# Two transformer layers on one core: paced bias blocks, softmax scaling and low weight parts on other engines, new step orders

## The chip, the cores and the metric

The kernel runs on one NeuronCore of a Trainium2 chip. Its engines work side by side, each on a queue of its own: TensorE (PE, matrix products into PSUM; its weight loads are PEld), VectorE (DVE), ScalarE (ACT), GpSimd (POOL) and SyncE (SP, which here only issues DMAs). They wait for each other by semaphores. The metric is the device time of one launch in microseconds (us), the median over several runs.

## The reference

Two layers over 512 latent tokens and 256 context tokens of width 1024 (`DEPTH = 2`). Layer 0 mixes tokens by differential attention (8 heads), layer 1 by neighbourhood attention (16 heads, a window of 8 rows by 16 columns of the token grid, with a learned bias per relative position, and all context tokens). Each is followed by an MLP. Context tokens go the same way, except after the last layer.

```
for i in range(DEPTH):
    mod_l = jnp.split((jax.nn.silu(c) @ w_mod[i] + b_mod[i])[:, None, :], N_MOD, axis=-1)
    mod_c = jnp.split((jax.nn.silu(c_ctx) @ w_mod[i] + b_mod[i])[None, None, :], N_MOD, axis=-1)
    h_l = modulate(rms_norm(x, norm1_g[i]), mod_l[0], mod_l[1])
    h_c = modulate(rms_norm(ctx, norm1_g[i]), mod_c[0], mod_c[1])
    ...
    x = x + mod_l[2] * y_l
    x = x + mod_l[5] * squared_relu_mlp(modulate(rms_norm(x, norm2_g[i]), mod_l[3], mod_l[4]), w_mlp1[i], w_mlp2[i])
    ...

# neighbourhood_mixer, one row of queries (layer 1)
s_loc = jnp.einsum('bqhd,brkhd->bhqrk', q_row, k_band).astype(jnp.float32) * ATTN_SCALE
bias = rpb[:, row_off][:, :, col_bias_idx].transpose(0, 2, 1, 3)
s_loc = jnp.where(col_in[None, None, :, None, :], s_loc + bias[None].astype(jnp.float32), -jnp.inf)
s_ctx = jnp.einsum('bqhd,bkhd->bhqk', q_row, k_c).astype(jnp.float32) * ATTN_SCALE
prob = jax.nn.softmax(jnp.concatenate([s_loc.reshape(...), s_ctx], axis=-1), axis=-1)
```

## The kernel before

**Products in parts.** Every large product is made of three PE passes over split operands: a value is held as a high part, which ACT copies from the raw float32 into the rounded type, and a low part, the difference between the two. `wraw` (L125) issues the DMA of a raw weight piece on SP, `wsplit` (L135) makes the high part on ACT (L140) and the low part on POOL unless another engine is named (L141). Raw pieces go through two buffers R.

**Stages.** After a start that sets up modulation and the first head, layer 0's eight heads run until about 434 us of the profile, then its output projection until about 550, its MLP until about 1176, layer 1's attention in eight groups of two heads until about 1547, its projection until about 1582, and its MLP to the end.

**Order of the work.** In the attention stages PE, SP and POOL keep the order in which the code is written; that order comes from strings of steps. `run` walks a string: `w` fetches a weight piece for the next head or group, `c` splits it, `Q` is the query, key and value product and its normalisation, `U` the transposes of queries and keys, `S` the scores with the softmax, `T` the transposes of the probabilities, `V` the product with the values. A prime marks the head or group before the one that is being begun. `P`, `X`, `B` belong to the output projection: a step of it, the split of a head's attention output, the gates. `m` and `n` are the modulation of the next layer. CYCLE1 is the string of layer 1's groups, LAST1 that of the last, END0 and END1 are the ends of the two attention stages. Elsewhere a scheduler orders instructions by its own estimate.

**Layer 1.** `group1` has the steps: `qk_normed` (a power of the mean square on POOL at L287, then the product with it on DVE at L414), `turn` (U: L623, L625, splits at L427 to L441), `scores` (S: products L645, bias added at L648, maximum L651, exponential L652, and the two halves scaled by the reciprocal of their sums on DVE, L656), `turned` (T: L675, high part L676 on ACT, low part L677 on DVE), `weigh` (V: L690).

**Bias blocks.** Layer 1's bias, 48 blocks of 128x256, is prepared during layer 0's MLP by `bias1`: a load, an addition of the window mask on POOL (L582), and a store to DRAM (L584). Two blocks are begun at each call of `sideB`, twice per chunk of the MLP, from the fourth call on; load and addition are one step, the store the next. The tiles are tagged OT, of which there are two. No order is written out here, and the scheduler places the bias work as early as its tiles allow.

**Buffers.** A tag opened on both sides of memory (left, right) is dealt out in turn. W1, layer 1's weights, has four buffers left and two right, and `b.turns["W1"] = 1` makes the count begin at the third. With it group 7's four pieces lie in two left and two right buffers. When the last group begins, the right two are closed, and W and ST (the projection's first weights and fetched attention outputs) are opened in their place.

**PSUM** has eight banks, dealt out in the order of a table per stage: PS_MLP0 has D0 and D1 in banks 0 to 3, A in 4 and 5, B in 6 and 7; PS_ATTN1 has B in 0 and 1, S in 2 to 4, A in 5 to 7. The last down product of an MLP uses A only, and the transposes L319 of the normalised rows for layer 1 use B.

## Time and profile before

| | |
|---|---|
| median of 3 runs | 1964.28 us (1960.87 to 1968.24) |
| profiled execution | 1957.72 us, span of its instructions 1955.9 us |
| granted TensorE clock, mean | 0.973 |
| PE busy | 1798.0 us of the span, 92% |
| DVE, ACT, POOL busy | 1164.7, 810.6, 804.8 us |

The profile is one execution taken by the hardware profiler. A busy time is the time in which an engine has an instruction under way, a wait is named by the instruction that ended it (`PE PA L623 <- DVE Y L414`: PE waited at line 623, writing PA, for DVE's result Y of line 414). The granted clock is the share of TensorE's full speed that the chip allowed in a stretch. Line numbers are those of the kernel before; after the change, lines further down are numbered 4 to 14 higher.

### The profile page before, as it was taken

Reading aid. Unit: us, or ns where it says so; the run is one execution under the profiler, and the core shown is the slowest. Engines: PE = TensorE matmul, PEld = TensorE weight load, DVE = VectorE, ACT = ScalarE, POOL = GpSimd, SP = SyncE. Lnnn points to the kernel's source line nnn. Section 1 sums busy time; section 2 is a strip of 40 time slices with the busy share of each in tenths; the row PEclk is TensorE's granted clock in tenths of the full one; section 3 lists DMA queues with packets and bytes.
Section 4 is the critical chain, followed back from the end, with each engine's and each line's share of the span. In section 5 each row is a group of like instructions: output and inputs, shape, how many; then the busy total and the mean of one; then the engine's idle time right before and its main releaser. Section 6 shows DMA issues by size and latency. Waiting matters only on the chain.

```text
span 1955.9 us, 27154 instructions
## 1 busy us (share of the span) xinstructions
PE 1798.0 (92%) x10256; PEld 1571.0 (80%) x10256; DVE 1164.7 (60%) x2194; ACT 810.6 (41%) x1822; POOL 804.8 (41%) x684
## 2 busy tenths in 40 slices
PE   6789999998878899999999998999887989999998
PEld 5778888886667788888888887888887778888886
DVE  4487787887463234333433585888886764444456
ACT  4476666675232122122122145566665443222321
POOL 3655566652443333223222343433433334434443
PEclk9999999998988999999999998999998899999999
DMA  8122222224555643233232121121112322323332
GB/s 319 41 82 76 85 84 84 87 82 144 157 132 129 152 145 120 96 122 117 107 116 87 57 97 66 62 79 55 62 63 87 112 88 89 106 86 95 100 98 75
DMA packets 66500, 197.61 MB, mean 101 GB/s; under 512 B 8193, under 2 KB 23489, under 8 KB 60225
## 3 DMA queue, kind: packets, MB, share of 16 engines
q1 hardware_dynamic: 58608, 186.03, 29.7%
q10 hardware_dynamic: 7760, 9.85, 1.4%
q8 instruction: 80, 1.31, 0.3%
q14 instruction: 52, 0.42, 0.1%
HBM read 180.74 MB, written 15.11 MB: 100 GB/s over the span
## 4 chain that ended last, share of the span: by engine, by line
PE 61%; DVE 13%; DMA 10%; issue 5%; POOL 5%; ACT 5%; POOLq 0%; SPq 0%; ACTq 0%; DVEq 0%
PE PD L816 19%; PE PA L851 11%; PE PB L851 9%; PE PA L399 8%; DMA OT<-in_rpb_dram 4%; PE PA L736 3%; DMA bias<-OT 2%; PE PA L248 2%; PE PS L508 2%; PE PB L543 2%; DMA R<-in_wqa_dram 2%; POOL W L141 2%; POOL SQ L287 2%; DVE Y L414 2%; PE PB L690 1%
## 5 line engine op out<-in xcount | busy, mean ns | idle before, releaser
L141 POOL TENSOR_TENSOR W<-R,W 128x1024 fp32r<-128x1024 f32 (+1 forms) x170 | 401.6, 2372 | 536.4 <-ACT W L140 536.1
L816 PE MATMUL PD<-Q,W 128*128 128x384 f32 (+2 forms) x1992 | 398.0, 347 | 15.4 <-POOL W L141 12.9
L816 PEld LDWEIGHTS PD<-Q,W 128*128 128x128 f32 x1992 | 346.9, 189 | 47.4 <-POOL W L141 13.6
L140 ACT ACTIVATE W<-R 128x1024 fp32r<-128x1024 f32 (+1 forms) x172 | 172.4, 1020 | 493.3 <-PE PA L851 198.2
L851 PE MATMUL PA<-W,H 128*128 128x512 f32 x1080 | 279.4, 398 | 4.1 <-POOL W L141 2.7
L851 PEld LDWEIGHTS PA<-W,H 128*128 128x128 f32 x1080 | 203.6, 191 | 52.6 <-issue 4.5
L825 DVE TENSOR_TENSOR N<-N 128x768 f32<-128x768 f32 (+1 forms) x64 | 66.4, 1039 | 285.3 <-ACT N L821 177.0
L851 PE MATMUL PB<-W,H 128*128 128x512 f32 x840 | 210.1, 392 | 0.0
L851 PEld LDWEIGHTS PB<-W,H 128*128 128x128 f32 x840 | 158.2, 189 | 33.6
L399 PE MATMUL PA<-W,Q 128*128 128x384 f32 (+1 forms) x1008 | 171.9, 324 | 6.8 <-DVE H L610 5.6
L399 PEld LDWEIGHTS PA<-W,Q 128*128 128x128 f32 x1008 | 158.6, 191 | 9.4 <-DVE H L610 6.6
L287 POOL TENSOR_TENSOR SQ<-SQ,half 128x4 f32<-128x4 f32 (+1 forms) x96 | 95.0, 990 | 163.2 <-DVE SQ L412 162.3
L399 PE MATMUL PA<-WB,H 128*128 128x384 f32 x576 | 110.0, 343 | 9.8 <-DVE Q L460 9.8
L828 DVE SCALAR_TENSOR_TENSOR H<-N,H 128x768 fp32r<-128x768 f32 (+1 forms) x64 | 95.2, 1490 | 24.5 <-ACT H L827 23.8
L399 PEld LDWEIGHTS PA<-WB,H 128*128 128x128 f32 x576 | 100.0, 191 | 10.9 <-DVE Q L460 10.4
L736 PE MATMUL PA<-W,H 128*128 128x512 f32 x384 | 98.1, 407 | 3.8 <-DVE T L741 3.8
L862 DVE TENSOR_TENSOR H<-PA,H 128x512 f32<-128x512 f32 x78 | 53.8, 690 | 70.4 <-PE PA L851 70.4
L816 PE MATMUL PD<-H,W 128*128 128x512 f32 (+1 forms) x408 | 93.7, 378 | 0.7 <-DVE SA L281 0.7
L414 DVE SCALAR_TENSOR_TENSOR Y<-Y,SQ 128x256 f32<-128x256 f32 (+1 forms) x96 | 76.9, 805 | 24.6 <-POOL SQ L287 24.1
L736 PEld LDWEIGHTS PA<-W,H 128*128 128x128 f32 x384 | 72.8, 195 | 21.6 <-DVE T L741 5.3
L508 PE MATMUL PS<-Q,Q 128*128 128x256 f32 (+1 forms) x320 | 68.9, 347 | 21.3 <-ACT E L514 10.3
L816 PEld LDWEIGHTS PD<-H,W 128*128 128x128 f32 x408 | 73.7, 188 | 15.9 <-DVE H L325 0.9
(207 smaller groups left out, 3005.1 us busy)
## 6 DMA issues: line engine op xcount, KB each, us to landing
R<-in_w_dram SPq DMA_DIRECT2D x128, 512.0 KB
M<-in_wmod_dram SPq DMA_DIRECT2D x48, 1024.0 KB
R<-in_wqa_dram SPq DMA_DIRECT2D x32, 384.0 KB
R<-in_wqb_dram SPq DMA_DIRECT2D x32, 384.0 KB
OT<-in_rpb_dram SPq DMA_DIRECT2D x48, 128.0 KB
bias<-OT SPq DMA_DIRECT2D x48, 128.0 KB
X<-bias SPq DMA_DIRECT2D x8, 768.0 KB
R<-in_woa_dram SPq DMA_DIRECT2D x8, 512.0 KB
```

Of the source, the lines that this page charges most:

```text
L140: nc.scalar.activation(w[:, 0, :n], raw, AF.Copy)
L141: (eng or nc.gpsimd).tensor_sub(w[:, 1, :n], raw, w[:, 0, :n].bitcast(F32))
L287: nc.gpsimd.tensor_tensor(r, ss, self.half[:, :n], op=ALU.pow)
L399: nc.tensor.matmul(acc[:, :n], hT[kt][:, x, P * i:P * i + P], w[kt // 2][:, y, o:o + n], start=(kt == 0 and p == 0), stop=(kt == KT - 1 an ...
L414: nc.vector.scalar_tensor_tensor(xn, xn, 1.0, r[:, :, None].to_broadcast([P, ns, 64]), op0=ALU.mult, op1=ALU.mult)
L508: nc.tensor.matmul(s[:, c0:c1], q[:, m, P * i:P * i + P], k[:, m, c0:c1], start=p == 0, stop=p == 1)
L736: nc.tensor.matmul(ps, oHL[h][:, x, c:c + P], w[h // 2][:, y, 512 * (h % 2):512 * (h % 2) + 512], start=(first and h == hs[0] and p == 0), ...
L816: nc.tensor.matmul(ps[:, at:at + b1 - b0], w[kt // 4][:, x, o:o + P], hT[kt][:, y, b0:b1], start=(kt == 0 and p == 0), stop=(kt == KT - 1 ...
L825: nc.vector.tensor_mul(r, r, r)
L828: nc.vector.scalar_tensor_tensor(u[:, 1, :], r, 1.0, u[:, 0, :].bitcast(F32), op0=ALU.mult, op1=ALU.subtract)
L851: nc.tensor.matmul(ps, hd[:, x, P * i - c0:P * i - c0 + P], w[f][:, y, 512 * n:512 * n + 512], start=(f == 0 and p == 0), stop=(f == len(h ...
L862: nc.vector.tensor_add(av, ps, av)
```

## The change

It has five parts.

1. **Bias blocks.** The tiles take tag Y, of which there are six. Load, addition and store are three steps, and each is tied to the engine's last weight work: load and store are issued right behind the last raw weight load on SP, the addition right behind the last low part on POOL. `sideB` advances up to four begun blocks and begins two more at every call, from the first.
2. **Engines in layer 1.** The low parts of groups 1 to 7 are made by DVE instead of POOL (28 subtractions). Of the two scalings of a softmax one goes to ACT, the other to POOL (32 each; 64 on DVE before).
3. **Fetches.** The DMA that fetches an attention output for the projection is a step `x` of its own, ahead of the split `X`.
4. **Step orders.** In CYCLE1 and LAST1 U4' of a group runs behind the next group's Q0 instead of ahead of it, T2' comes ahead of Q5b, V2' ahead of U0 and U2. END0, LAST1 and END1 have the new fetches, and splits spread among other steps. The start of W1's count falls away, so that group 7's weights lie in the four left buffers.
5. **PSUM.** PS_ATTN1 has A first (banks 0 to 2), PS_MLP1 is mirrored to fit.

```diff
-END0 = """S1' O2'' O3'' X0 X1 V4'' T0' U4' n1' V5'' T1' X2 S2' X3 O4'' P0a O5'' X4 V0' S3' T2' X5 B0 P0b P1a V1'
...
+END0 = """x0 x1 x2 x3 S1' O2'' O3'' V4'' T0' U4' n1' V5'' T1' X0 S2' X1 O4'' x4 X2 x5 P0a O5'' V0' S3' X3 T2' X4 B0
+X5 P0b P1a V1' O0' S4' m0 P1b V2' O1' x6 P2a T3' n0 P2b T4' S5' P3a O2' P3b V3' V4' m1 T5' P4a O3' n1 X6
...
-CYCLE1 = """w0 w1 Q0 Q1 c0 w2 S0' Q2a S1' c1 w3 Q2b Q3a T0' Q3b S2' T1' Q4a S3' V0' Q4b V1' Q5a c2 Q5b c3 T2' T3' U0
-U2 V2' V3' U4"""
+CYCLE1 = """w0 w1 Q0 U4' Q1 c0 w2 S0' Q2a S1' c1 w3 Q2b Q3a T0' Q3b S2' T1' Q4a S3' V0' Q4b V1' Q5a c2 T2' Q5b c3 T3'
+V2' U0 U2 V3'"""
-LAST1 = """Q0 Q1 c0 S0' Q2a S1' Q2b X0 Q3a T0' Q3b X1 S2' T1' Q4a S3' V0' X2 Q4b V1' Q5a Q5b T2' T3' U0 U2 V2' V3'
-X3 U4"""
-END1 = """c1 S0' S1' X4 T0' S2' c2 T1' P2a V0' S3' P3a X5 B0 V1' P4a T2' V2' P2b T3' X6 P3b V3' P4b P5a P5b"""
+LAST1 = """Q0 U4' Q1 c0 x0 x1 S0' Q2a S1' Q2b X0 x2 Q3a T0' Q3b X1 x3 S2' T1' Q4a S3' V0' X2 Q4b V1' Q5a T2' Q5b T3'
+V2' U0 U2 V3'"""
+END1 = """c1 X3 x4 U4' S0' S1' x5 T0' S2' X4 c2 T1' P2a V0' S3' X5 P3a B0 V1' P4a T2' V2' x6 P2b T3' X6 P3b V3' P4b
+P5a P5b"""
...
-PS_ATTN1 = dict(B=2, S=3, A=3)
-PS_MLP1 = dict(D0=1, A=2, B=2, D1=1)
+PS_ATTN1 = dict(A=3, S=3, B=2)
+PS_MLP1 = dict(A=2, B=2, D1=1, D0=1)
...
-        self.nc.sync.dma_start(raw, src)
+        self.last["SP"] = self.nc.sync.dma_start(raw, src)
...
+    def behind(self, eng):
+
+        return self.tc.issue_after(self.last[eng].ins)
...
-        (eng or nc.gpsimd).tensor_sub(w[:, 1, :n], raw, w[:, 0, :n].bitcast(F32))
+        low = (eng or nc.gpsimd).tensor_sub(w[:, 1, :n], raw, w[:, 0, :n].bitcast(F32))
+        self.last["POOL" if eng is None else "other"] = low
...
-        b = self.sbt('OT', [P, 256])
+        b = self.sbt('Y', [P, 256])
...
-        nc.sync.dma_start(b, bass.AP(tensor=rpb.tensor, offset=off, ap=[[1, 16], [32, 8], [1, 256]]))
-        nc.gpsimd.tensor_add(b, b, self.mask[:, j])
+        with self.behind("SP"):
+            nc.sync.dma_start(b, bass.AP(tensor=rpb.tensor, offset=off, ap=[[1, 16], [32, 8], [1, 256]]))
         yield
-        nc.sync.dma_start(self.bias[h // 2, :, h % 2, j], b)
+        with self.behind("POOL"):
+            nc.gpsimd.tensor_add(b, b, self.mask[:, j])
+        yield
+        with self.behind("SP"):
+            nc.sync.dma_start(self.bias[h // 2, :, h % 2, j], b)
         yield
...
-            for jj in range(2):
-                nc.vector.tensor_scalar_mul(e[:, jj, 0:512], e[:, jj, 0:512], r[:, jj:jj + 1])
+            nc.scalar.activation(e[:, 0, 0:512], e[:, 0, 0:512], AF.Copy, scale=r[:, 0:1])
+            nc.gpsimd.tensor_scalar_mul(e[:, 1, 0:512], e[:, 1, 0:512], r[:, 1:2])
...
+        def fetch(h):
+            st = raws[h] = self.sbt('ST' if 'ST' in self.room else 'N', [P, ntok])
+            nc.sync.dma_start(st, oT[h])
+
         def split(h, eng):
-            st = self.sbt('ST' if 'ST' in self.room else 'N', [P, ntok])
-            nc.sync.dma_start(st, oT[h])
+            st = raws.pop(h)
...
+                       "x": lambda n: proj["fetch"](int(n)),
...
-                sides.append(1)
-                while begun:
-                    next(begun.pop(0))
-                for _ in range(2 if len(sides) > 3 else 0):
-                    if units:
-                        begun.append(units.pop(0))
-                        next(begun[-1])
+
+                for u in begun:
+                    next(u, None)
+                del begun[:2 if len(begun) == 4 else 0]
+                for u in units[:2]:
+                    begun.append(units.pop(0))
+                    next(begun[-1])
...
-        b.turns["W1"] = 1
...
-                    w.setdefault(g, []).append(b.wsplit(raws.pop((g, k)), 768, tag="W1"))
+                    w.setdefault(g, []).append(b.wsplit(raws.pop((g, k)), 768, eng=nc.vector, tag="W1"))
```

Where this moves instructions, the engines' queues show. First SP at the start of layer 0's MLP. R are raw weight pieces (`in_w_dram` holds the MLP's, `in_wmod_dram` the modulation's), OT and Y the bias tiles, `in_rpb_dram` the table they are read from, `bias` where they are stored. Before:

```order
L581 DMA OT_7500<-in_rpb_dram 128x1x256
L128 DMA R_6670<-in_w_dram 128x1024
L584 DMA bias<-OT_7357 128x256
L584 DMA bias<-OT_7500 128x256
L581 DMA OT_7503<-in_rpb_dram 128x1x256
L581 DMA OT_7632<-in_rpb_dram 128x1x256
L128 DMA R_6675<-in_w_dram 128x1024
L584 DMA bias<-OT_7503 128x256
L584 DMA bias<-OT_7632 128x256
L581 DMA OT_7635<-in_rpb_dram 128x1x256
L581 DMA OT_7778<-in_rpb_dram 128x1x256
```

The same place now:

```order
L129 DMA R_6670<-in_w_dram 128x1024
L129 DMA R_6675<-in_w_dram 128x1024
...
L129 DMA R_6978<-in_w_dram 128x1024
L129 DMA R_6983<-in_w_dram 128x1024
L588 DMA Y_6974<-in_rpb_dram 128x1x256
L588 DMA Y_6976<-in_rpb_dram 128x1x256
L588 DMA Y_7102<-in_rpb_dram 128x1x256
L588 DMA Y_7104<-in_rpb_dram 128x1x256
...
L129 DMA R_7106<-in_w_dram 128x1024
L129 DMA R_7111<-in_w_dram 128x1024
...
L594 DMA bias<-Y_6974 128x256
L594 DMA bias<-Y_6976 128x256
```

Between the first two weight pieces of the MLP there stood bias loads and stores, each store behind a POOL addition; now six pieces go ahead of the first bias load (two of them left out here), and stores come a call or two behind their loads.

Next PE at the change from layer 0's MLP to layer 1. L851 (now L864) is the last down product, PA<-W,H; L319 (now L325) transposes normalised rows N into PB; L399 (now L405) is the Q step of group 0. Before:

```order
L851 MATMUL PA_11088<-W_10754,H_10434 128x512 x3
L851 MATMUL PA_11088<-W_10759,H_10489 128x512 x3
L851 MATMUL PA_11088<-W_10764,H_10670 128x512 x3
L851 MATMUL PA_11088<-W_10769,H_10725 128x512 x3
L319 MATMUL PB_11020<-ident,N_10998 128x128
L851 MATMUL PA_11106<-W_10754,H_10434 128x512 x3
...
L319 MATMUL PB_11188<-ident,N_11140 128x128
L319 MATMUL PB_11188<-ident,N_11151 128x128
...
L319 MATMUL PB_11201<-ident,N_11151 128x128
L399 MATMUL PA_11251<-H_10772,Q_6654 128x256 x3
```

Now:

```order
L405 MATMUL PA_11251<-H_10772,Q_6655 128x256 x3
L864 MATMUL PA_11088<-W_10754,H_10444 128x512 x3
L864 MATMUL PA_11088<-W_10759,H_10499 128x512 x3
L864 MATMUL PA_11088<-W_10764,H_10670 128x512 x3
L864 MATMUL PA_11088<-W_10769,H_10725 128x512 x3
L405 MATMUL PA_11251<-H_10777,Q_6656 128x256 x3
L405 MATMUL PA_11251<-H_10777,Q_6657 128x256 x3
L325 MATMUL PB_11020<-ident,N_10998 128x128
L864 MATMUL PA_11106<-W_10754,H_10444 128x512 x3
L864 MATMUL PA_11106<-W_10759,H_10499 128x512 x3
L864 MATMUL PA_11106<-W_10764,H_10670 128x512
L325 MATMUL PB_11033<-ident,N_10998 128x128
```

Q steps stood behind all transposes; now they lie between the down products and the transposes.

Last DVE at the end of a cycle of layer 1. L677 (now L687) makes the low part N of the transposed probabilities PB, which the V step reads; L414 (now L420) scales queries and keys Y; L610 (now L620) is the low part of the values; L146 in the new order is the low part W of a weight piece R. Before:

```order
L412 TENSOR_REDUCE SQ_11862<-sq_83 128x4
L698 TENSOR_TENSOR T_11844<-PB_11869,T_11844 64x256
L414 SCALAR_TENSOR_TENSOR Y_11859<-Y_11859,SQ_11864 128x256
L610 TENSOR_TENSOR H_11562<-PA_11882,H_11562 128x2x64
L677 TENSOR_TENSOR N_11923<-PB_11925,N_11923 128x512
L412 TENSOR_REDUCE SQ_11913<-sq_83 128x4
L677 TENSOR_TENSOR N_11924<-PB_11932,N_11924 128x512
L414 SCALAR_TENSOR_TENSOR Y_11910<-Y_11910,SQ_11915 128x256
L677 TENSOR_TENSOR N_11939<-PB_11941,N_11939 128x512
L677 TENSOR_TENSOR N_11940<-PB_11948,N_11940 128x512
```

Now:

```order
L418 TENSOR_REDUCE SQ_11862<-sq_83 128x4
L708 TENSOR_TENSOR T_11844<-PB_11869,T_11844 64x256
L146 TENSOR_TENSOR W_11895<-R_11611,W_11895 128x768
L420 SCALAR_TENSOR_TENSOR Y_11859<-Y_11859,SQ_11864 128x256
L146 TENSOR_TENSOR W_11936<-R_11679,W_11936 128x768
L687 TENSOR_TENSOR N_11898<-PB_11900,N_11898 128x512
L687 TENSOR_TENSOR N_11899<-PB_11907,N_11899 128x512
L620 TENSOR_TENSOR H_11540<-PA_11882,H_11540 128x2x64
L146 TENSOR_TENSOR W_12112<-R_12015,W_12112 128x768
L418 TENSOR_REDUCE SQ_11929<-sq_83 128x4
L687 TENSOR_TENSOR N_11939<-PB_11941,N_11939 128x512
L687 TENSOR_TENSOR N_11940<-PB_11948,N_11940 128x512
```

Two of the four subtractions stand directly ahead of the L687 pairs of T2' and T3', and two ahead of L420.

More of the change, by code (lines that the diff above doesn't have):

```diff
@@ L73, in __init__ @@
         self.dram = pool("dram", 1, space=DRAM)
-        self.room, self.turns = {}, {}
+        self.room, self.turns, self.last = {}, {}, {}
     BUFS = {"H": 8, "Q": 8, "E": 2, "X": 2, "Y": 6, "T": 2, "SQ": 12, "SA": 12, "SO": 8, "C4": 1}
@@ L721, in project @@
         ntok = T - P * t0
-        oHL, w0, x0, acc = {}, [], [], {}
+        oHL, raws, w0, x0, acc = {}, {}, [], [], {}
         gate = {}
+        def fetch(h):
+            st = raws[h] = self.sbt('ST' if 'ST' in self.room else 'N', [P, ntok])
+            nc.sync.dma_start(st, oT[h])
         def split(h, eng):
-            st = self.sbt('ST' if 'ST' in self.room else 'N', [P, ntok])
-            nc.sync.dma_start(st, oT[h])
+            st = raws.pop(h)
             u = oHL[h] = self.sbt(tag_o[h // 4], [P, 2, ntok], F32R)
@@ L790, in end @@
                     self.modulated(xns, (i - 1, i), l, 1, hT, tag_p)
-        return dict(weights=weights, begin=begin, split=split, step=step, split_last=split_last, end=end)
+        return dict(weights=weights, begin=begin, fetch=fetch, split=split, step=step, split_last=split_last, end=end)
     def mlp(self, l, t0, xh, hT, tag, mid, done, side):
@@ L982, in hybrid_block @@
             w1 = []
-            units, begun, sides = [b.bias1(u) for u in range(6 * GROUPS1)], [], []
+            units, begun = [b.bias1(u) for u in range(6 * GROUPS1)], []
             def sideB():
@@ L1021, in hybrid_block @@
                 own = {"P": lambda n: proj["step"](2 * int(n[0]) + (n[1] == "b")), "B": lambda _: proj["begin"](),
+                       "x": lambda n: proj["fetch"](int(n)),
                        "X": lambda n: proj["split"](int(n), nc.gpsimd)}
```

3 lines of the change are left out of this document (1 added, 2 removed).

## The prediction

> **What bounds the kernel now.** I read the page first: TensorE (PE) is busy for 92% of the span, so the most that better feeding can give is some 158 us.
>
> ```profile
> span 1955.9 us, 27154 instructions
> PE 1798.0 (92%) x10256; PEld 1571.0 (80%) x10256; DVE 1164.7 (60%) x2194; ACT 810.6 (41%) x1822; POOL 804.8 (41%) x684
> ```
>
> Then the busy time by stretch, to see where those 158 us lie. Columns: stretch, its length, busy time of PE, weight loads, DVE, ACT and POOL, the granted clock, the DMA share.
>
> ```profile
> 434.00:450.00 16.00, 9.58 (x53) 7.59 (x51) 12.65 (x30) 13.39 (x34) 11.82 (x12) 0.84 0.90 324
> 500.00:550.00 50.00, 41.47 (x176) 32.77 (x174) 27.00 (x49) 10.99 (x25) 23.16 (x20) 0.93 0.52 119
> 550.00:600.00 50.00, 37.61 (x261) 34.76 (x260) 29.90 (x58) 21.69 (x41) 24.49 (x22) 0.90 0.63 152
> 600.00:650.00 50.00, 43.04 (x219) 38.39 (x218) 13.76 (x19) 9.38 (x11) 14.54 (x15) 0.90 0.51 108
> 650.00:700.00 50.00, 41.70 (x226) 36.54 (x225) 13.85 (x19) 7.76 (x10) 22.56 (x17) 0.93 0.66 181
> 880.00:916.70 36.70, 36.70 (x210) 32.02 (x209) 13.83 (x20) 7.99 (x10) 9.87 (x4) 1.00 0.31 114
> 1254.22:1295.47 41.25, 37.01 (x258) 35.59 (x258) 34.59 (x75) 25.41 (x66) 16.13 (x18) 1.00 0.20 65
> 1500.00:1550.00 50.00, 36.84 (x190) 31.56 (x191) 35.56 (x71) 25.40 (x56) 21.06 (x21) 0.77 0.43 148
> ```
>
> Layer 0's MLP in its steady part (a chunk from 880) is PE alone: 36.70 of 36.70. The holes are elsewhere: 36.2 us from 500 to 700, where the first MLP chunks run; 4.2 us in each cycle of layer 1; 13.2 us from 1500 to 1550, where layer 1's attention ends and the clock falls to 0.77; 6.4 us of 16 from 434, where layer 0's output projection begins. Who is waited for, over the span (total, times, longest):
>
> ```profile
> PE PS L319 <- DVE N L302: 19.4, 6, 10.6
> PE PD L816 <- POOL W L141: 12.9, 2, 7.0
> PE PB L690 <- DVE N L677: 10.9, 7, 1.8
> PE PA L623 <- DVE Y L414: 8.9, 5, 3.4
> PE PA L399 <- DVE H L610: 5.6, 5, 1.1
> PE PS L645 <- ACT H L437: 4.7, 1, 4.7
> ```
>
> **Bias blocks (500 to 700): 25 us.** The chain of waits from 504 on is a string of the bias load, its add and its store, and the timeline shows what stands behind it:
>
> ```profile
> 507.50 3.79 DMA bias<-OT
> 511.30 4.32 DMA OT<-in_rpb_dram
> 515.78 0.75 POOL OT L582
> 516.54 1.70 DMA bias<-OT
> ...
> 552.81 0.15 DVE L281 TENSOR_SCALAR SA<-SA 128x1 f32<-128x1 f32 x1
> 561.32 0.72 POOL L582 TENSOR_TENSOR OT<-OT,C 128x256 f32<-128x256 f32 x1 [3.99 <-DMA OT<-in_rpb_dram]
> 563.48 0.55 POOL L287 TENSOR_TENSOR SA<-SA,half 128x1 f32<-128x1 f32 x1
> 564.06 2.55 DVE L302 TENSOR_SCALAR N<-E,SA 128x512 f32<-128x512 f32 x1 [11.11 <-POOL SA L287]
> ```
>
> DVE had the variance at 552.96. The power (L287) needs 0.55 us, but in POOL's queue it stands behind four bias adds, each waiting for its load, and starts 10.5 us late. That is the longest wait, 10.6, of PE's transposes L319 for the normalised rows. SP's queue has the same jam: two buffers, so a load waits for a store, which waits for an add, and the weight loads L128 stand between them. That is the 12.9 us for low parts L141. In the new order SP has six weight loads ahead of the first bias load; then two units per side call, loaded, added and stored in three successive calls. No issuing engine then waits for a transfer of the same call. The same 48 loads, 48 stores and 48 adds remain.
>
> Gain: 10.6 + 12.9 = 23.5 us. What is late next is the chain itself: with the variance in hand, 0.55 for the power and 2.55 for the first L302, so some 3 us of the 10.6 stay: 20.5. Beside waits there is the clock: the four stretches lack 0.07, 0.10, 0.10 and 0.07 of 50 us, 17 us of pulses in all, part of them while PE idles. I take 4.5 us of it as coming back: 25. Bounds: 18 (20.5 less 2.5 for a first weight load that is late in any order) and 32 (36.2 idle less those 3 and about one more).
>
> **The steady MLP loop: 0.** The adds go to later chunks instead: four per chunk of 36.70 us, 4 × 0.75 = 3.0 us on POOL, which is busy 9.87 of it. SP's cover is this:
>
> ```profile
> 888.48 22.91 SPq L128 DMA_DIRECT2D R<-in_w_dram  x3
> 907.50 2.01 ACT L140 ACTIVATE W<-R 128x1024 fp32r<-128x1024 f32 x2 [17.35 <-PE PA L851]
> ```
>
> A weight load goes out at 888.48, and its use at 907.50 is released by PE freeing the buffer, not by the DMA. About 19 us lie between; I estimate 4 to 6 for a load (the bias loads above took 4.3). So SP may be held over 10 us before PE sees it. Without the cover each of 24 calls would pay a store, 1.7: 41 us. Bounds −4, a tenth of that, and 0.
>
> **Start of the projection in layer 0: 5 us.** The fetches (DMA) become steps ahead, and six splits that stood in two crowds are spread. From 434 to 450 ACT, POOL and DVE are all busy for 11.8 to 13.4 of 16 us and PE idles for 6.4. The splits don't vanish, so I take 5; bounds 0 (they crowd the next heads) and 8 (with the clock, 0.84).
>
> **Start of layer 1: 8.5 us.** The waits of the last transposes, and PE's own rows:
>
> ```profile
> PE PB L319 <- ACT Y L322: 3.7, 5, 1.2
> ...
> 1183.71 1.54 PE L319 MATMUL PB<-ident,N 128*128 128x128 f32 x6 [1.13 <-DVE N L302]
> 1187.45 23.52 PE L399 MATMUL PA<-H,Q 128*128 128x256 f32 x144
> 1215.79 0.33 PE L623 MATMUL PA<-ident,Y 128*128 128x128 f32 x1 [3.42 <-DVE Y L414]
> ```
>
> With A's three banks first, group 0's Q steps don't share banks with the last down products; the new order has three of the six Q steps among these and the transposes L319, where before all 144 matmuls came after 1187.45. The transposes wait 3.7 for ACT and 1.13 for DVE, 4.8 us in all, and the Q matmuls can fill that: with the slowed matmuls around it I take 5. The 3.42 wait before U4' goes too, as the next group's Q0 (a sixth of the 23.52 above, 3.9 us) now stands ahead of it: 8.4, said as 8.5. Bounds 4 (the U4' wait only) and 12.
>
> **Layer-1 cycles: 3 us.** Removed from DVE are the two scalings of each softmax, from POOL the low parts:
>
> ```profile
> L656 DVE TENSOR_SCALAR E<-E,SA 128x512 f32<-128x512 f32 x64 | 28.6, 489 | 0.6
> L676 ACT ACTIVATE N<-PB 128x512 fp32r<-128x512 f32 x64 | 36.0, 599 | 11.0 <-PE PB L675 11.0
> 1328.60 1.85 POOL L141 TENSOR_TENSOR W<-R,W 128x768 fp32r<-128x768 f32 x1
> 1328.66 2.08 DVE L414 SCALAR_TENSOR_TENSOR Y<-Y,SQ 128x256 f32<-128x256 f32 x1 [0.66 <-POOL SQ L287]
> 1333.66 0.84 ACT L140 ACTIVATE W<-R 128x768 fp32r<-128x768 f32 x1 [1.03 <-DMA R<-in_wqb_dram]
> 1508.35 0.43 DVE L414 SCALAR_TENSOR_TENSOR Y<-Y,SQ 128x256 f32<-128x256 f32 x1
> ```
>
> Per cycle DVE loses 8 × 0.489 = 3.9 us and takes four subtractions of 128x768; ACT gains four scalings at about 0.6 (L676's shape) = 2.4, giving 27.8 of 41.25; POOL loses 4 × 1.85 = 7.4 and takes four scalings. The price of such a scaling on POOL isn't in this trace: 0.73 (L582, half the size) to 1.85 (L141); I take 1.0. The subtraction on DVE isn't either: below 1.0, by L414 alone at 0.43 for a third of the size, to 2.1, stretched; I take 1.05. DVE comes out even at least, since L414 takes 2.08 under a POOL subtraction and 0.43 without.
>
> The Trainium skill (SBUF — State Buffer, "Who interferes with whom") says that a DVE instruction with two SBUF inputs and a GpSimd instruction that reads SBUF block each other for the whole instruction. The trace agrees for L414, 2.08 against 0.43. By that rule the moved subtractions would hold up POOL's powers in turn; it is the second rival below.
>
> PE's waits in a cycle are 4.2 us: for L677 up to 1.8, for H L610 about 1.1, the rest in pieces. The second goes, as U4' now runs between Q0 and Q1: −1.1. Before V2' the T2' step's new place ahead of Q5b gives L677 for it a start of several us, so that only the L677 of T3' is late: I take −0.4 of the 1.8. Against it two of the new subtractions stand before the L677 in DVE's queue, each behind a DMA and ACT (the load behind 1333.66 was awaited for 1.03): one of them, 1.05 as its price here, comes on the path. Together −0.45 for a cycle of 41.25, times 7: 3. Bounds −10 (cycle 42.7, if both L677 come behind a late weight) and +9.
>
> **End of layer 1: 8 us.**
>
> ```profile
> 1493.39 7.16 SPq L727 DMA_DIRECT2D ST<-oT  x3
> 1498.93 1.27 POOL L730 TENSOR_TENSOR H<-ST,H 128x512 fp32r<-128x512 f32 x1
> 1500.15 1.19 POOL L287 TENSOR_TENSOR SQ<-SQ,half 128x4 f32<-128x4 f32 x1
> ...
> L287 POOL TENSOR_TENSOR SQ<-SQ,half 128x4 f32<-128x4 f32 x80 | 83.9, 1049 | 135.8 <-DVE SQ L412 135.4
> ```
>
> The fetches ST reuse the right W1 buffers, which hold group 7's weights until its last Q step, so they go out at 1493 and their splits fall into the final chain: POOL's L730 stands before the power that releases L414 and so L623: of its 8.9 us of waits 3.4 lie at layer 1's start, and most of the other 5.5 here. Without the turn of W1 those weights are in the left buffers, and fetches and splits begin with the last group's first steps. U4' of the last group again has Q0 ahead of it. I count 4 of those 5.5, 2 for the splits that leave ACT's and POOL's queues ahead of S0' (two L730 are 2.5) and 2 of clock, since 0.77 over 50 us lacks 11.5 us of pulses: 8. Left are the 4.7 us from U4' to S0' and the softmax before T0', now with a scaling on POOL behind low parts of up to 2.4. Bounds 3 and 12. MLP of layer 1: unchanged, 0 ± 2.
>
> **Sum:** 25 + 0 + 5 + 8.5 + 3 + 8 = 49.5 us. The profiled execution took 1957.72 (span 1955.9), so 1908; the median, 1964.28, is 6.6 above it, and I carry that: 1964.3 − 49.5 = 1914.8, said as 1914.
>
> **The rivals.**
> *Bias jam only shortened.* For it: from 500 to 700 weights, normalisation and projection evictions press the same engines (DVE 27 to 30 of 50 us until 600), and a removed wait uncovers the next. If half of the 25 us and the low ends of the two starts come (12 + 2 + 5 + 3 + 5 = 27): 1937. Against it: the string of rpb transfers is itself the chain there.
>
> *POOL's powers blocked by DVE.* In layer 1 a subtraction of 1.05 us may hold off a power (1.19 above, against a mean of 1.05) and with it L420, U and S. Four per cycle, 1.05 each, 7 cycles: −29 in place of the 3 gained: 49.5 − 32 = 17, 1947. For it: 2.08 against 0.43 in reverse order. Against it: of the four only c2 and c3 stand next to a power that PE awaits; with these two alone the gain is 32, 1932.
>
> *Slower: DVE held by weight transfers.* DVE now takes a subtraction that waits for SP, DMA and ACT, and everything behind it in order waits too: L677 before V2', L620 before Q1, the row maxima before S. At 1333.66 ACT awaited such a load for 1.03. Each load that comes late by d costs PE d, four times a cycle, seven cycles: the 46.5 us of the other parts are used up at d = 1.7. At d = 2.5 the kernel takes 1964 − 46.5 + 70 = 1988. Against it: only w0 and w1 are issued just before use; w2 and w3 have over 10 us.
>
> *More than I count.* The upper ends of bias, both starts and the end of layer 1 (32 + 7 + 11 + 11, and 6 from the cycles): 67, 1897 or somewhat below.
>
> The Trainium skill (TensorE: Matmul & The Clock Gate, Part 1) puts the half clock down to idle windows of about 3.4 us. Here 0.77 stands where waits of 4.7 occur, which agrees; by it closing the two long waits before 600 would return all of those 17 us of pulses, and 1914 would be about 1902, inside the last case.
>
> **How the numbers follow.** The forecast, 1900 to 1928: 0.52. Jam only shortened: 0.19. Powers blocked: 0.10. More: 0.10. Slower by held DVE: 0.05; a mixture of small losses with almost no gain: 0.04. About what a measurement of this kernel can tell from no change is 0.5%, here 1954.5 to 1974.1. Slower takes 0.04 of the held-DVE case, same its other 0.01 with the mixture and 0.02 from blocked powers: 0.07. Faster has the rest, 0.89. The range 1888 to 1944 leaves out about 0.06 below, and 0.13 above.
>
> **What would show it.** Right: no bias rows in the chain between 500 and 700; L319's wait for L302 under 9 us in all and L816's for the low part gone; 36.7 us per steady chunk as before; Q matmuls before 1187 less the gain; cycles of about 40.7; the clock of the end of layer 1 near 0.9. Wrong: cycles of 42 or more with PE waiting for L687 or L620 behind a subtraction that awaits a weight; a steady chunk over 37.5; the bias terms replaced by waits for evictions or X splits of the same size.

## The result, and the profile after

The changed kernel takes 1917.09 us, the median of four runs (1913.11 to 1917.39), beside 1962.57 for the kernel before; the ratio is 0.9759, 95% interval 0.9734 to 0.9785. The profiled execution took 1917.39 us, its span is 1915.6.

The page of the kernel after, its head:

```profile
span 1915.6 us, 27143 instructions
PE 1796.2 (94%) x10256; PEld 1572.7 (82%) x10256; DVE 1132.3 (59%) x2158; ACT 834.9 (44%) x1854; POOL 808.8 (42%) x688
```

The same stretches as in the prediction (columns as there), then a cycle of layer 1 and the end of its attention, from group 6's first V step to the projection's first product:

```profile
434.00:450.00 16.00, 10.33 (x74) 7.51 (x72) 11.85 (x32) 12.59 (x36) 7.27 (x11) 0.93 0.61 222
500.00:550.00 50.00, 47.40 (x216) 38.26 (x215) 30.92 (x59) 18.14 (x39) 15.68 (x11) 1.00 0.19 58
550.00:600.00 50.00, 47.20 (x323) 44.61 (x324) 31.86 (x58) 21.35 (x35) 23.16 (x13) 1.00 0.53 143
600.00:650.00 50.00, 50.00 (x271) 43.37 (x270) 19.43 (x26) 9.41 (x12) 13.65 (x9) 1.00 0.37 121
650.00:700.00 50.00, 50.00 (x297) 44.50 (x296) 16.14 (x23) 11.27 (x15) 19.20 (x12) 1.00 0.46 158
850.00:886.70 36.70, 36.70 (x216) 32.01 (x208) 13.82 (x18) 8.02 (x11) 13.38 (x9) 1.00 0.42 144
1240.87:1283.56 42.69, 39.36 (x261) 38.29 (x260) 30.33 (x71) 28.60 (x70) 14.88 (x18) 0.92 0.19 62
1450.94:1485.97 35.03, 25.76 (x144) 23.40 (x143) 20.82 (x50) 25.17 (x56) 16.24 (x17) 0.75 0.31 112
```

The 36.2 us of idle PE between 500 and 700 are 5.4, and the clock there is 1.00. The steady chunk still takes 36.70, with 3.5 us more on POOL (13.38 against 9.87). A cycle of layer 1 has become longer, 42.69 against 41.25, and its clock fell from 1.00 to 0.92. The end of layer 1's attention is shorter, 35.03 against 42.32 for the same work, but its clock is 0.75, not the 0.9 that I had named. PE's waits, over the whole span:

```profile
PE PB L700 <- DVE N L687: 17.6, 8, 2.8
PE PA L405 <- DVE H L620: 6.3, 8, 2.5
PE PS L325 <- DVE N L308: 5.1, 4, 2.5
PE PS L655 <- ACT H L443: 5.0, 5, 2.3
```

L325's wait for the normalised rows fell from 19.4 to 5.1, and the 12.9 us for POOL's low parts in the first chunks are off the list. The wait before the V steps, L700 for L687, rose from 10.9 to 17.6.

A sign of being right that the prediction named came: the bias loads, stores and adds, 73% of the chain of waits from 505 to 700 before, stand nowhere in it now. A sign of being wrong came as well: cycles near 42 us, in which PE waits for L687 behind a subtraction that awaits a weight.

From the starts of PE's matmuls in the two profiled executions, stage by stage:

| stage | before | after | gain | foreseen |
|---|---|---|---|---|
| start to the last Q matmul of layer 0 | 432.1 | 434.0 | −1.9 | 0 |
| to the first up product of its MLP | 123.5 | 115.5 | +8.0 | 5 (fetches and splits), part of 25 (bias) |
| to its last up product | 582.3 | 550.8 | +31.5 | rest of 25 |
| to group 0's first V step | 101.6 | 97.9 | +3.7 | 8.5 |
| six cycles, to group 6's first V step | 246.1 | 252.8 | −6.7 | +3 (seven cycles) |
| to the first up product of layer 1's MLP | 96.8 | 90.8 | +6.0 | 8 |
| to the last down product | 368.5 | 368.9 | −0.3 | 0 |

The first row is not the change's: programs that are alike up to there took 432.1 to 439.5 us in the profiled executions of this case. Later stages vary less, but they vary: the six cycles of the kernel before took 246.1 us here and 249.5 in the run with bias pacing alone, which has the same cycles; those of the changed kernel took 252.8 here and 249.8 in the run with layer 0's end in its old order. So the loss in the cycles is between nothing and 6.7 us. Sums of whole runs tell less than the lengths of stages, and both are given below. The intervals are of ratios to the kernel before.

### The profile page after: what moved, and what is told of

Same layout as the page of the kernel before. It is cut to its first block, busy times and chain, and to the rows that moved or that the text cites. A ratio compares the mean times of both kernels' runs of the same rounds, so it can differ in the third digit from the quotient of the medians.

```text
span 1915.6 us, 27143 instructions
## 1 busy us (share of the span) xinstructions
PE 1796.2 (94%) x10256; PEld 1572.7 (82%) x10256; DVE 1132.3 (59%) x2158; ACT 834.9 (44%) x1854; POOL 808.8 (42%) x688
## 4 chain that ended last, share of the span: by engine, by line
PE 71%; DVE 12%; ACT 5%; DMA 5%; issue 4%; POOL 3%; ACTq 0%; SPq 0%; POOLq 0%; DVEq 0%
PE PD L829 22%; PE PA L405 11%; PE PA L864 11%; PE PB L864 9%; PE PA L749 4%; PE PB L700 2%; PE PA L254 2%; PE PS L514 2%; PE PB L549 1%; DMA R<-in_wqa_dram 1%; DMA R<-in_wqb_dram 1%; PE PS L655 1%; ACT E L520 1%; PE PQ L395 1%; ACT W L145 1%
## 5 line engine op out<-in xcount | busy, mean ns | idle before, releaser
L146 POOL TENSOR_TENSOR W<-R,W 128x1024 fp32r<-128x1024 f32 x142 | 351.4, 2485 | 541.2 <-ACT W L145 541.1
L864 PE MATMUL PA<-W,H 128*128 128x512 f32 x1080 | 275.5, 394 | 4.6 <-POOL W L146 2.9
L864 PEld LDWEIGHTS PA<-W,H 128*128 128x128 f32 x1080 | 200.2, 188 | 51.5 <-issue 4.5
L864 PE MATMUL PB<-W,H 128*128 128x512 f32 x840 | 209.3, 391 | 0.0
L864 PEld LDWEIGHTS PB<-W,H 128*128 128x128 f32 x840 | 157.4, 188 | 33.3
L405 PE MATMUL PA<-W,Q 128*128 128x384 f32 (+1 forms) x1008 | 172.4, 323 | 4.2 <-DVE H L620 3.8
L405 PEld LDWEIGHTS PA<-W,Q 128*128 128x128 f32 x1008 | 157.1, 189 | 6.1 <-DVE H L620 5.5
L293 POOL TENSOR_TENSOR SQ<-SQ,half 128x4 f32<-128x4 f32 (+1 forms) x96 | 93.9, 979 | 132.6 <-DVE SQ L418 131.7
L405 PE MATMUL PA<-WB,H 128*128 128x384 f32 x576 | 110.5, 344 | 9.9 <-DVE Q L466 9.9
L405 PEld LDWEIGHTS PA<-WB,H 128*128 128x128 f32 x576 | 100.5, 191 | 11.0 <-DVE Q L466 10.5
L520 ACT ACTIVATE E<-PS,SA 128x768 f32<-128x768 f32 (+1 forms) x96 | 72.7, 758 | 27.9 <-DVE SA L519 25.5
```

The lines of the kernel that those rows point to most:

```text
L146: low = (eng or nc.gpsimd).tensor_sub(w[:, 1, :n], raw, w[:, 0, :n].bitcast(F32))
L293: nc.gpsimd.tensor_tensor(r, ss, self.half[:, :n], op=ALU.pow)
L405: nc.tensor.matmul(acc[:, :n], hT[kt][:, x, P * i:P * i + P], w[kt // 2][:, y, o:o + n], start=(kt == 0 and p == 0), stop=(kt == KT - 1 an ...
L520: nc.scalar.activation(e[:, m, :nk], s, AF.Exp, bias=mx[:, 0:1], accum_out=sm[:, m:m + 1])
L864: nc.tensor.matmul(ps, hd[:, x, P * i - c0:P * i - c0 + P], w[f][:, y, 512 * n:512 * n + 512], start=(f == 0 and p == 0), stop=(f == len(h ...
```

## The experiments

Theory A was that the bias transfers alone made the holes of 500 to 700 us, and that the cycles of layer 1 grew because a subtraction on DVE that awaits a weight stands ahead of L687. The timeline of one cycle after the change shows the place:

```profile
1291.12 5.35 SPq L129 DMA_DIRECT2D R<-in_wqb_dram  x3
1294.28 0.84 ACT L145 ACTIVATE W<-R 128x768 fp32r<-128x768 f32 x1 [0.44 <-DMA R<-in_wqb_dram]
1295.16 0.96 DVE L146 TENSOR_TENSOR W<-R,W 128x768 fp32r<-128x768 f32 x1 [0.99 <-ACT W L145]
1295.34 1.06 ACT L686 ACTIVATE N<-PB 128x512 fp32r<-128x512 f32 x2
1296.37 1.28 DVE L687 TENSOR_TENSOR N<-PB,N 128x512 fp32r<-128x512 f32 x2
1297.10 0.73 PE L700 MATMUL PB<-N,H 128*128 128x256 f32 x4 [2.77 <-DVE N L687]
```

A weight load issued at 1291.12 reaches ACT at 1294.28; the eviction of T3' (L686) stands behind its high part on ACT, and L687 behind its low part on DVE, where DVE idled 0.99 us for it. PE waits 2.77. By the order of the steps this is the first piece of the next group (`w0`), whose split the scheduler has put ahead of the last eviction of this one. The rival: the softmax scaling, which takes 1.57 us on POOL where DVE took 0.49, delays the T steps. The groups of four cycles after the change:

```profile
L666 POOL TENSOR_SCALAR E<-E,SA 128x512 f32<-128x512 f32 x16 | 25.1, 1569 | 31.6 <-DVE SA L664 25.3 <-PE PA L405 6.3
L665 ACT ACTIVATE E<-E,SA 128x512 f32<-128x512 f32 x16 | 11.6, 725 | 5.0 <-DVE SA L664 5.0
L146 DVE TENSOR_TENSOR W<-R,W 128x768 fp32r<-128x768 f32 x16 | 15.3, 954 | 6.5 <-ACT W L145 6.5
L420 DVE SCALAR_TENSOR_TENSOR Y<-Y,SQ 128x256 f32<-128x256 f32 x16 | 6.7, 418 | 0.0
L293 POOL TENSOR_TENSOR SQ<-SQ,half 128x4 f32<-128x4 f32 x16 | 16.4, 1027 | 40.4 <-DVE SQ L418 40.3
```

**Weight parts pinned behind the evictions.** The only change to the changed kernel:

```diff
+    self.last["ACT"] = nc.scalar.activation(pT[hb][:, 0, :], ps, AF.Copy)
+    self.last["DVE"] = nc.vector.tensor_sub(pT[hb][:, 1, :], ps, pT[hb][:, 0, :].bitcast(F32))
...
+    with ExitStack() as es:
+        if "DVE" in b.last:
+            es.enter_context(b.behind("ACT"))
+            es.enter_context(b.behind("DVE"))
+        w.setdefault(g, []).append(b.wsplit(raws.pop((g, k)), 768, eng=nc.vector, tag="W1"))
```

> The changed kernel, with one thing more: in layer 1 the high parts (ACT) and low parts (DVE) of the next group's weights are queued behind the last eviction of a T step (L686 on ACT, L687 on DVE), so that none of them stands ahead of that eviction. Nothing is left out. Theory A (DVE and ACT are held by a weight transfer: the 2.8 us wait before V2' in each cycle is L687 standing behind a subtraction that awaits its weight): the wait for L687 falls from 14.7 us in six cycles to under 5, the granted clock in the cycles returns to 1.00, cycles are 39.5 to 40.5 us instead of 41.7 to 42.7, and the kernel takes 1900 to 1908 us. Rival B (the softmax scaling, 1.57 us on POOL, makes the T steps late): cycles within 0.4 us of 42.2, 1914 to 1920 us.

1897.62 us, ratio 0.9668 (0.9645 to 0.9691), clear of the changed kernel's 0.9759. A cycle, and the waits over five cycles:

```profile
1239.09:1277.32 38.23, 36.65 (x261) 35.68 (x260) 29.96 (x71) 28.55 (x70) 14.88 (x18) 1.00 0.21 70
...
PE PB L700 <- DVE N L687: 4.9, 5, 1.0
PE PA L405 <- DVE H L620: 2.2, 5, 0.5
```

38.2 us, shorter than theory A's number, with the clock at 1.00. Between pinned and not, only the place of the weight parts in the queues differs, so that place cost the changed kernel 3.4 to 4.6 us in each of the first five cycles. The sums over all six cycles, of the kernel before, the changed one and the pinned one:

```profile
sum 246.12, PE 221.93 PEld 213.69 DVE 202.74 ACT 151.40 POOL 91.00; mean PE 36.99 PEld 35.61 DVE 33.79 ACT 25.23 POOL 15.17
sum 252.80, PE 230.57 PEld 223.55 DVE 180.90 ACT 172.74 POOL 94.32; mean PE 38.43 PEld 37.26 DVE 30.15 ACT 28.79 POOL 15.72
sum 233.80, PE 221.86 PEld 215.70 DVE 178.95 ACT 172.53 POOL 94.26; mean PE 36.98 PEld 35.95 DVE 29.82 ACT 28.75 POOL 15.71
```

PE's idle time is the sum less its busy time: 24.2, 22.2 and 11.9 us. So the pins took 10.3 us of idle time out of the changed kernel and 8.7 of busy time, the latter by the clock, since the matmuls are the same. Against the kernel before, the changed one does not wait more in sum; it is longer by 8.6 us of busy time at the lower clock.

**Low weight parts back on POOL.**

```diff
-                    w.setdefault(g, []).append(b.wsplit(raws.pop((g, k)), 768, eng=nc.vector, tag="W1"))
+                    w.setdefault(g, []).append(b.wsplit(raws.pop((g, k)), 768, tag="W1"))
```

> The changed kernel with layer 1's low weight parts back on POOL; the softmax scalings stay on ACT and POOL, and so do all step orders. Nothing is left out. Theory A (DVE held by a weight transfer): the wait before V2' is shorter than 2.8 us; in its place the products with the power (L420) are stretched from 0.42 to about 2 us while POOL makes a low part, as before the change; cycles 40.8 to 41.8, 1906 to 1914 us. Rival B (softmax scaling on POOL): POOL now has both, cycles stay at 42.2 or grow, 1917 to 1925 us.

1919.32 us, 0.9773 (0.9750 to 0.9796): theory A's number was too low. As it said, the wait before V2' fell (4.9 us in six cycles) and L420 was stretched, here in one cycle and over six:

```profile
L420 DVE SCALAR_TENSOR_TENSOR Y<-Y,SQ 128x256 f32<-128x256 f32 x5 | 5.3, 1068 | 1.3 <-POOL SQ L293 1.3
...
PE PA L405 <- DVE H L620: 13.6, 6, 2.3
```

What it missed is that a new wait of 2.3 us comes with that: Q1 for L620, after DVE was held 2.04 us in one L420 by a low part on POOL. Cycles stay near 42.0. Time and cycles are those that rival B gave, but none of PE's waits in these cycles is for the scaling L666; the new order with the low parts alone on POOL was not run. The wait for L687 fell with the high parts still unpinned on ACT, so it was DVE's part that mattered.

**Softmax scalings back on DVE.**

```diff
-    nc.scalar.activation(e[:, 0, 0:512], e[:, 0, 0:512], AF.Copy, scale=r[:, 0:1])
-    nc.gpsimd.tensor_scalar_mul(e[:, 1, 0:512], e[:, 1, 0:512], r[:, 1:2])
+    for jj in range(2):
+        nc.vector.tensor_scalar_mul(e[:, jj, 0:512], e[:, jj, 0:512], r[:, jj:jj + 1])
```

> The changed kernel with both softmax scalings back on DVE (two of about 0.49 us), the low weight parts still on DVE. Nothing is left out. Theory A: the wait before V2' stays, since its cause is the weight transfer; cycles within 0.5 us of 42.2, 1914 to 1921 us. Rival B: the T steps come earlier by about 0.6 us each, cycles of 41.2 or less, 1905 to 1911 us.

1915.40 us, 0.9755 (0.9736 to 0.9774): no difference, and the cycle is that of the changed kernel.

```profile
1242.87:1285.63 42.76, 39.35 (x260) 38.28 (x259) 33.24 (x79) 26.18 (x66) 8.85 (x14) 0.92 0.19 62
```

The rival has fallen for the cycles. **With pinned parts and scalings on DVE** (both edits above):

> The kernel with pinned weight parts in layer 1, and both softmax scalings back on DVE. Nothing is left out. Theory A (the scalings' place matters only at the end of layer 1, where T waits for POOL's): cycles within 0.4 us of 38.1 to 38.4, the end of layer 1 2 to 4 us shorter, 1893 to 1897 us. Rival B (with the weight wait gone DVE is the next bound, 30 us of 38 plus 4): cycles of 39 or more, 1899 to 1906 us.

1901.02 us, 0.9680 (0.9651 to 0.9708). Cycles of 38.1 to 38.4, so DVE is no bound there; but from group 6's first V step to the projection's first product it took 36.0 us, and 35.6 with the scalings on ACT and POOL: the expected 2 to 4 us at the end did not come. (Without the pin the scalings on DVE gave 33.7 against 35.0; but another execution with the same end, that with layer 0's end in its old order, took 34.25, so they are worth a microsecond there at most.)

**Bias pacing alone,** the first part of the change put into the kernel before:

> The kernel before, with the bias part of the change alone: tag Y, three steps, each tied to the last weight load on SP or low part on POOL, from the first side call on. Nothing is left out. Theory A (the string of bias transfers was the whole cause of the holes from 500 to 700 us): the first 200 us of layer 0's MLP gain 28 to 33 us as in the changed kernel, 1929 to 1936 us, and everything after it keeps its lengths. Rival B (part of that gain came from the spread of the splits before it and needs it): 15 to 24 us, 1938 to 1948 us.

1922.37 us, 0.9787 (0.9762 to 0.9813): more than theory A's number. From the last Q matmul of layer 0 to the first up product it needs 115.2 us, from there to the last up product 552.0: gains of 8.3 and 30.3, nearly all that the changed kernel has there (8.0 and 31.5). Its first stretches, and then both gains as one stretch, in the kernel before and in this run:

```profile
500.00:550.00 50.00, 46.65 (x212) 37.37 (x210) 32.50 (x60) 17.71 (x39) 15.78 (x11) 1.00 0.18 59
550.00:600.00 50.00, 47.22 (x316) 44.87 (x317) 30.27 (x57) 21.45 (x35) 22.00 (x12) 0.97 0.49 138
...
432.10:1137.83 705.73, 659.62 (x3615) 568.12 (x3615) 318.14 (x475) 181.47 (x297) 233.93 (x148) 0.97 0.39 121
434.22:1101.42 667.20, 650.88 (x3616) 561.96 (x3615) 317.27 (x475) 181.44 (x297) 240.46 (x148) 0.99 0.39 128
```

PE's idle time falls from 46.1 to 16.3 us there, its busy time by 8.7.

**Layer 0's end in its old order,** with each fetch directly ahead of its split:

```diff
-END0 = """x0 x1 x2 x3 S1' O2'' O3'' V4'' T0' U4' n1' V5'' T1' X0 S2' X1 O4'' x4 X2 x5 P0a O5'' V0' S3' X3 T2' X4 B0
+END0 = """S1' O2'' O3'' x0 X0 x1 X1 V4'' T0' U4' n1' V5'' T1' x2 X2 S2' x3 X3 O4'' P0a O5'' x4 X4 V0' S3' T2' x5 X5 B0 P0b P1a V1'
...
```

> The changed kernel with the step order of before at the end of layer 0's attention: each fetch directly ahead of its split, splits in their old places. Nothing is left out. Theory A (with bias paced, the spread of fetches and splits is worth little, since the run with bias pacing alone reached layer 0's MLP as early as the changed kernel): first up product within 1.5 us of 549.4, 1915 to 1919 us. Rival B (the spread is worth the 5 us that I gave it): first up product 553 to 556, 1920 to 1924 us.

1917.85 us, 0.9770 (0.9753 to 0.9787); 115.2 us from the last Q matmul to the first up product, against 115.5: theory A. The spread is worth nothing that shows.

**PSUM tables of before** in the changed kernel:

```diff
-PS_ATTN1 = dict(A=3, S=3, B=2)
-PS_MLP1 = dict(A=2, B=2, D1=1, D0=1)
+PS_ATTN1 = dict(B=2, S=3, A=3)
+PS_MLP1 = dict(D0=1, A=2, B=2, D1=1)
```

> The changed kernel with the PSUM tables of before (B, S, A in layer 1; D0, A, B, D1 in its MLP); all else as changed. Nothing is left out. Theory A (the banks let Q steps of group 0 fill holes among the last transposes): no Q matmul before the last transposes, the stretch from the last up product of layer 0's MLP to group 0's first V step grows from 97.9 us by 3 to 5, 1919 to 1923 us. Rival B (the gain there comes from U4' standing behind Q0, and the Q steps only change places): the stretch stays within 1 us, 1916 to 1918 us.

1921.64 us, 0.9789 (0.9770 to 0.9808). The stretch to group 0's first V step is 103.0 us, 5.1 longer, as theory A has it. The waits there:

```profile
PE PB L325 <- ACT Y L328: 4.8, 5, 2.3
PE PB L325 <- DVE N L308: 4.0, 1, 4.0
```

In the changed kernel these transposes wait 2.3 us for ACT and not for DVE, but Q3 then waits 2.5 for L620, the low part of the values.

**Layer 1's end in its old order,** U4' and the buffers as changed:

```diff
-LAST1 = """Q0 U4' Q1 c0 x0 x1 S0' Q2a S1' Q2b X0 x2 Q3a T0' Q3b X1 x3 S2' T1' Q4a S3' V0' X2 Q4b V1' Q5a T2' Q5b T3'
-V2' U0 U2 V3'"""
-END1 = """c1 X3 x4 U4' S0' S1' x5 T0' S2' X4 c2 T1' P2a V0' S3' X5 P3a B0 V1' P4a T2' V2' x6 P2b T3' X6 P3b V3' P4b
-P5a P5b"""
+LAST1 = """Q0 U4' Q1 c0 S0' Q2a S1' Q2b x0 X0 Q3a T0' Q3b x1 X1 S2' T1' Q4a S3' V0' x2 X2 Q4b V1' Q5a Q5b T2' T3' U0 U2 V2' V3'
+x3 X3"""
+END1 = """c1 U4' S0' S1' x4 X4 T0' S2' c2 T1' P2a V0' S3' P3a x5 X5 B0 V1' P4a T2' V2' P2b T3' x6 X6 P3b V3' P4b P5a P5b"""
```

> The changed kernel with the step order of before for the last group and the end of layer 1's attention: each fetch directly ahead of its split, splits in their old places, T2' and V2' in theirs; U4' stays behind Q0 and S0', and group 7's weights stay in the four left buffers. Nothing is left out. Theory A (spread splits and U4's place end the chain earlier): from group 6's first V step to the first output projection step 37 to 40 us in place of 35.0, 1919 to 1923 us. Rival B (the free right buffers alone did it): within 1 us of 35.0, 1916 to 1919 us.

1917.90 us, 0.9765 (0.9748 to 0.9783); 35.31 us to the projection's first product, against 35.03 and 34.25 in two executions of the changed end: rival B's number, so the splits' places are worth a microsecond at most. That the free buffers alone did it, as rival B had it, the next run does not bear out. **The turn of W1 alone** (one line taken from the kernel before):

```diff
-        b.turns["W1"] = 1
```

> The kernel before, with one line taken out: W1's count begins at the first buffer, so that group 7's weights lie in the four left buffers. All step orders as before. Nothing is left out. Theory A (the free right buffers alone shorten the end of layer 1, since the fetches go out earlier): from group 6's first V step to the first output projection step 36 to 39 us in place of 42.3, 1958 to 1961 us. Rival B (it needs U4' behind Q0 as well: the final chain is the power, the products with it, U4' and S0'): 41 to 43 us, 1963 to 1966 us.

1962.81 us, 0.9988 (0.9979 to 0.9998), and the stretch:

```profile
1495.79:1535.47 39.68, 26.71 (x145) 24.05 (x143) 28.95 (x60) 22.68 (x53) 16.84 (x17) 0.74 0.30 93
```

39.68 in place of 42.32, between the numbers of both theories: the buffers give 2.6 of the 7.3 us that this stretch gained. Where the other 4.6 come from stays open. Each other part of the change that bears on it, undone by itself, leaves the stretch short: the splits' places 35.3, low parts on POOL 34.6, scalings on DVE 33.7, the PSUM tables 34.7, and U4' ahead of the last group's Q0 34.2 (the run after this one). In the trace of this run DVE takes 3.24 us for two scalings L656 from 1524.83 on, and PE then waits 3.5 for L439 behind them; whether that is the difference was not tested. A kernel with the changed order and the old turn was not run.

**The cycles in their old order:**

```diff
-CYCLE1 = """w0 w1 Q0 U4' Q1 c0 w2 S0' ... Q5a c2 T2' Q5b c3 T3' V2' U0 U2 V3'"""
+CYCLE1 = """w0 w1 Q0 Q1 c0 w2 S0' ... Q5a c2 Q5b c3 T2' T3' U0 U2 V2' V3' U4"""
```

> The changed kernel with the step order of before in the cycles of layer 1 (U4' ahead of Q0, T2' behind c3, U0 and U2 ahead of V2'), and U4' of the last group ahead of its Q0. The engines stay as changed. Nothing is left out. Theory A (low parts ahead of the evictions on DVE hold V2' in either order; the new orders gain what stands ahead of U4'): cycles of 42.5 to 44, group 0's U4' waits again, 1922 to 1932 us. Rival B (the new order made the cycles longer): cycles of 41 or less, 1905 to 1915 us.

The last group's string loses its `U4'` behind `Q0` too. 1913.93 us, 0.9747 (0.9724 to 0.9770): here theory A was wrong. The second cycle and the fifth:

```profile
1239.13:1280.16 41.03, 36.89 (x261) 35.68 (x260) 29.79 (x71) 28.42 (x70) 14.93 (x18) 1.00 0.20 65
...
1362.21:1405.15 42.94, 38.16 (x261) 37.17 (x259) 29.78 (x71) 28.41 (x70) 14.92 (x18) 0.96 0.19 62
```

The first four cycles take 40.8 to 41.1 us with the clock at 1.00, and L700 waits 1.9 to 2.1 in them; the wait of 2.8 that theory A had comes in the fifth alone, which takes 42.9 at 0.96. At group 0 U4' waits 2.5 us for L420 again and the stretch to the first V step takes 101.0, 3 us more than in the changed kernel. So the new order helped the start by some 3 us. In the cycles, as long as the weight parts were not pinned, it cost 0.5 to 1 us each: the first five take 41.4 us on average here, 42.3 in the changed kernel, and 41.9 in the runs with layer 0's and with layer 1's end in the old order. It cost that by the clock, for the one cycle of these fifteen at 1.00 took 40.3. In the time of the whole run no difference shows: the intervals overlap. With the pin the new order gives 38.2; the old order with the pin was not run.

**Pinned, with U0 and U2 ahead of V2'** in CYCLE1 and LAST1 (`T3' U0 U2 V2' V3'`):

> The kernel with pinned weight parts in layer 1, and in its cycles U0 and U2 ahead of V2', as before the change. Nothing is left out. Theory A (the 1.15 us left before V2' is the eviction of T3''s first tile, which frees V2''s bank; transposes put there cover it): cycles 37.2 to 37.8 in place of 38.1, 1890 to 1896 us. Rival B (U0 and U2 then wait for their product L420, or V3' takes over the wait): 38 or more, 1897 to 1903 us.

1894.68 us, 0.9649 (0.9635 to 0.9664), the lowest of all, though its interval overlaps that of the pin alone. A cycle, its waits over five, and the last group's cycle:

```profile
1236.60:1274.67 38.07, 36.80 (x260) 35.72 (x259) 30.09 (x71) 28.40 (x70) 14.91 (x18) 1.00 0.22 70
...
PE PA L405 <- DVE H L620: 4.2, 5, 0.8
PE PB L700 <- DVE N L687: 1.6, 5, 0.3
...
1388.80:1429.41 40.61, 37.40 (x260) 35.88 (x259) 29.55 (x69) 29.51 (x72) 19.92 (x21) 1.00 0.13 41
```

The wait before V2' went, as theory A said, and another took its place after U4' (rival B), so the cycles stayed; the gain is in the last group's, 40.6 against 42.8. **Pinning on ACT behind the exponentials too** (weight parts and the splits of layer 1):

> As the kernel with pinned weight parts and U0 and U2 ahead of V2', and in layer 1 the weight parts and the splits of attention outputs are queued on ACT behind the exponentials of the S step before them. Nothing is left out. Theory A (two splits on ACT, 1.15 us, stand ahead of the conversions of U4' and U2 in the last group, which S0' awaits): the cycle of the last group, 42.8 us, comes to 39 to 41.5, 1887 to 1893 us. Rival B (the conversions wait for each other, and the splits only fill the gaps): within 1 us of the kernel without it.

1903.65 us, 0.9686 (0.9670 to 0.9702). The last group's cycle is 40.5, no better, and the other cycles grew to 38.8, with S0' waiting up to 0.8 us: neither theory foresaw a loss.

## Why the prediction was right, and where it was off

The forecast of 1914 us was 3 us from the measured 1917.09. That it came so close is luck in part: 49.5 us were foreseen, 45.5 found by the medians and 40.3 from the start to the last down product of the two profiled executions, because one term was 14 us too small and others too large.

- **Bias blocks**: the mechanism held, the term was too small. 25 us were foreseen; pacing alone gives 8.3 + 30.3 = 38.6. The failed step is the sum over waits: I credited the two longest (23.5), took 3 off and returned 4.5 us of clock. In the stretch from the last Q matmul to the last up product PE waited 15.9 us for L302, 12.9 for the low parts and 2.3 for a modulation load; 1.7 of these 31.1 are left with pacing alone. The jam began earlier than I had looked, inside the projection, where POOL's powers stood behind bias adds too (4.7 of the 15.9). PE's idle time fell by 29.8, its busy time by 8.7. By the rule of the Trainium skill that I set beside it (TensorE: Matmul & The Clock Gate, Part 1) all 17 us of pulses return. The clock does (1.00, and 0.97 to 1.00 with pacing alone), but the 8.7 us that it was worth are nearer to my 4.5.
- **Fetches and splits in layer 0**: 5 foreseen, nothing found. Idle time in a crowded stretch was taken as this part's to win; its gain was that of the bias blocks.
- **Start of layer 1**: 8.5 foreseen, 3.7 found. Banks and U4' did what they should (5.1 and 3 us when undone one at a time), but the transposes still wait 2.3 us for ACT, and Q3 takes over with 2.5 us for L620. I had let the Q steps fill the holes without asking what the fourth of them waits for.
- **Cycles**: +3 foreseen, −6.7 found in this pair of executions, inside the stated bounds. The waits came out nearly as summed: PE's idle time fell by 2.0 us in six cycles, where 6 × 0.45 = 2.7 were foreseen. It is made up otherwise, though: the wait of the V steps for L687 rose from 1.8 us to between 2.6 and 2.8, while the waits of the T steps for the L677 before them (7.5 us in all) went. The failed step is the clock, which the term had not at all: PE's busy time grew by 8.6 us at 0.92 to 0.96. The place was that of the third rival, as the pins show, but not the price: a late load was to cost its delay in idle time, and idle time did not grow. My argument against it, that only `w0` and `w1` are issued just before use, left out that DVE takes `w0` of the next group ahead of this group's last eviction.
- **Powers blocked by DVE**: the rival was not put to the test in the changed kernel, where no power (L293) runs at the same time as a low part on DVE. With the pins five do, for 0.58 us each (one from 1250.99 to 1252.00 beside a low part from 1251.43 to 1252.38), and neither is longer for it than the others are: 1.01 and 0.95 us. The other half of that rule of the Trainium skill (SBUF — State Buffer, "Who interferes with whom") is plain: L420 takes 418 ns without low parts on POOL, and 1068 with them.
- **End of layer 1**: 8 foreseen, 6.0 found. Of the means named, the buffers give 2.6 us and the splits' places one at most; U4' behind Q0 shows nothing in this stretch, which is 34.2 us without it, and what gives the other 4.6 us stays open. The clock, of which I expected 2 us, hardly returned: it was 0.72 in this stretch before and is 0.75. The scaling on POOL stands before T there (PE waits 1.5 us for L666) but moving it back gave at most 1.3 us in one order and none in the other.
- **Steady MLP loop**: 0 foreseen and found; 400 to 1400 up products take as long as before. POOL's price for an add is 0.95 us now, not 0.75, and hidden. A POOL scaling is 1.57 us, not 1.0, and mostly hidden.

## What to carry to other kernels

When a string of small transfers appears in the chain of waits, cost the whole stretch that it holds up, from the first queue that it enters, not the longest waits in it. When work moves to an engine that keeps its order, look up what that work itself waits for, and pin it behind the instructions that the bottleneck awaits: here the same subtractions cost some 4 us more in a cycle ahead of L687 than behind it. More pins are not better: the same on ACT behind the exponentials cost 9 us again. A hole filled in one place should be followed to the next thing that is late.
